# Memory and its keys turned by VectorE and carried through DRAM, and h written in block order

## The chip, the cores and the metric

The kernel runs on one core of a Trainium2 chip. Its time is that of one execution on the device, in microseconds; several executions are timed, and their median counts. One further execution is recorded by the hardware profiler, and the rows in this document come from such records.

## The reference, cut to what matters

Two layers over x (256 rows of 1024, float32), with a memory of 256 rows of 1024 that both layers attend to:

```
for i in range(2):
    x = x + 0.5 * swiglu(rmsnorm(x, ffn1_norm[i]), w_gate, w_up, w_down)   # 1024 -> 2816 -> 1024
    proj = rmsnorm(x, mix_norm[i]) @ w_in[i]           # queries, keys, values, memory queries
    mkv = rmsnorm(mem, mem_norm[i]) @ w_mem_kv[i]      # 1024 -> 2 x 256
    k_m, v_m = split(mkv)
    k_m = rmsnorm(k_m per head of 64, mem_k_norm[i])   # 4 heads
    o_m = softmax(q_m k_m' / 8) v_m
    ...                                                # 12 self heads: biased (layer 0), differential (layer 1)
    x = x + concat(o_s, o_m) @ w_out[i]
    x = x + 0.5 * swiglu(rmsnorm(x, ffn2_norm[i]), ...)
```

## The kernel before

A matrix product takes its contraction along the partitions, so everything that is multiplied has to lie with its columns on the partitions: x, memory, the gated product h, the memory keys. Every float32 operand is split into a rounded part and a rest (`hi` and `lo`), and a product is three matmuls: hi x hi, hi x lo, lo x hi (`dense`, L383, L386, L389).

**Weights.** They come in chunks of 1 MB, in one fixed order: per FFN 22 gate/up chunks and 11 down chunks; in layer 0, behind the first FFN, four chunks of the memory's key and value weights for both layers, then the mixer's. `loader` sends each chunk into one of 3 raw buffers (L270); `split_hi` (ScalarE, L302) and `split_lo` (VectorE, L314) write it into one of 4 hi/lo buffers, in quarters. A raw buffer is free when the rest is written, a hi/lo buffer when TensorE has used the chunk for the last time. In the kernel before, the memory itself is a chunk too (1 MB, ahead of the down stage's last three), not split.

**Order of the work.** All instructions of all engines are put in order when the kernel is built, by a planner (`Flow`): threads (Python generators) yield a time or a condition, and a clock with fixed costs (0.216 us a matmul, and so on) says when each goes on. The splits and the loader are idle threads, taken when no other is ready. What the planner gives is the order in each engine's queue; the chip then runs each queue as its data come. `at[0]` is the number of the chunk that TensorE works on. Small loads go through a list (`later`): the loader sends one of them behind each chunk from number 5 on, and `loaded` waits until that is done and 8 us more:

```
if i > 4 and late_done[0] < len(late_loads):
    dst, src = late_loads[late_done[0]]
    late_done[0] += 1
    nc.sync.dma_start(out=dst, in_=src)
```

**Gate/up.** For each of 11 groups of 256 columns, TensorE fills two PSUM banks (`gu`, one for each 128 rows of x). `evac` applies the SiLU on ScalarE (L491), multiplies on VectorE into `h` (L494), and turns h in 32x32 blocks on VectorE into `hb` (L502). Blocks of 32 rows are then put in their places by a write to DRAM (`hd`, L508) and a read back (`hr`, L513), and split into `ht` (L519, L521) for the down stage.

**Down.** 11 chunks accumulate in four banks (`acc`); the last three (c = 8 to 10) are taken bank by bank, so that they stay in their buffers until nearly the end, while `finish` adds each finished half to x, turns it on TensorE (`xtp`), scales and splits it (`y`, `xh`, `xl`).

**Memory.** `memory_prep` is started in the first down stage, after chunk c = 6. It turns the memory chunk by 16 TensorE transposes (`mtp`, in packs), and for each layer splits it with that layer's gain into `memh` (ScalarE, L628) and `meml` (VectorE, L633). At the start of the first mixer, `memory_kv` multiplies it with the key and value weights for both layers (`kv`), normalises the keys (`kmn`, L590), turns them by TensorE (`kmtp`) and splits them into `km`. They are first used by the memory attention, at the end of the mixer (`S<-km`).

Of the kernel before, what the change touches and what calls it, by code (L numbers as in the profile page):

```python
# [12 lines left out]
F32 = mybir.dt.float32  # L13
# [4 lines left out]
ALU = mybir.AluOpType  # L18
# [124 lines left out]
def kernel(  # L143
# [94 lines left out]


    class Chunk:  # L240
        def __init__(self, parts, mem=False):
            self.parts, self.mem = parts, mem
# [10 lines left out]
    LAT = 1.5  # L253
    at = [0]

    def add_chunk(parts, uses=8, mem=False):
        c = Chunk(parts, mem)
        c.uses = uses
        c.index = len(chunks)
        chunks.append(c)  # L260
        return c
# [25 lines left out]

    def split_hi():
        for i, c in enumerate(chunks):
            if c.mem:  # L290
                continue
            yield lambda: c.raw is not None and hl_left[0] > 0
            hl_left[0] -= 1
            yield c.early or c.arrive
            c.hi = whl.tile([P, 2048], F32R, tag="hi", name=f"hi{i}")
            c.lo = whl.tile([P, 2048], F32R, tag="lo", name=f"lo{i}")
            for q in range(4):
                if q == 2:
                    yield c.arrive
                yield lambda: flow.free["A"] <= flow.now + SLACK or i <= at[0] + AHEAD  # L300
                sl = slice(q * 512, (q + 1) * 512)
                nc.scalar.copy(out=c.hi[:, sl], in_=c.raw[:, sl])  # L302
                c.hit[q] = flow.act(512)

    def split_lo():
        for i, c in enumerate(chunks):
            if c.mem:
                continue
            for q in range(4):
                yield lambda: c.hit[q] is not None  # L310
                yield c.hit[q]
                yield lambda: flow.free["V"] <= flow.now + SLACK or i <= at[0] + AHEAD
                sl = slice(q * 512, (q + 1) * 512)
                nc.vector.tensor_sub(c.lo[:, sl], c.raw[:, sl], c.hi.bitcast(F32)[:, sl])  # L314
                c.lot[q] = flow.dve(512)
            raw_left[0] += 1
# [21 lines left out]
    def plan_ffn(l, nm, wg, wu, wd):  # L338
        gu = []
        for g in range(NG):  # L340
            ids = []
            for c in range(2):
                pieces = 2 if len(chunks) < 2 else 1
                a = cols4(wg[l], c, g * 256, 256, 0, pieces)
                b = cols4(wu[l], c, g * 256, 256, 256, pieces)
                ids.append(add_chunk([q for ab in zip(a, b) for q in ab]))
            gu.append(ids)
        plan[l, nm, "gu"] = gu
        dn = []
        for c in range(NG):  # L350
            dn.append(add_chunk(rows2(wd[l], c)))
            if (l, nm) == (0, 1) and c == NG - 4:
                plan["mem"] = add_chunk(
                    [(lambda raw: raw.rearrange("p (b d) -> p b d", b=2), mem[0].rearrange("(b p) d -> p b d", p=P))],
                    mem=True)
        plan[l, nm, "dn"] = dn

    for l in range(DEPTH):
# [119 lines left out]
    def ffn(l, nm, xt, gc_next):  # L478
# [3 lines left out]
        def evac(g, ps, end):  # L482
# [3 lines left out]
            for tb in range(2):  # L486
                yield lambda: end[tb] is not None and xt.rt[tb] is not None
                yield end[tb]
                yield g2.has(3)
                sil = g2.take([P, 256], F32, "sil")  # L490
                nc.scalar.activation(sil, ps[tb][:, 0:256], AF.Silu, scale=xt.r[tb])  # L491
                yield flow.act(256)
                h = g2.take([P, 256], F32, "h")
                nc.vector.scalar_tensor_tensor(out=h, in0=ps[tb][:, 256:512], scalar=xt.r[tb], in1=sil,  # L494
                                               op0=ALU.mult, op1=ALU.mult)
                t = flow.dve(256, 0.06)
                g2.give()
# [4 lines left out]
                nc.vector.transpose(out=hb[:, :, tb].rearrange("p b f j -> p f b j"),  # L502
                                    in_=h.rearrange("p (f i b) -> p f b i", f=2, b=4))
                t = flow.dve(256, 0.05)
                g2.give()
            yield t
# [91 lines left out]
    kvres = {}  # L598
    mrs = [const.tile([P, 1], F32, name=f"mr{tb}") for tb in range(2)]

    def memory_prep():
        c = plan["mem"]
        yield lambda: c.arrive is not None
        yield c.arrive
        yield g4.has(4 * DEPTH)
        mr = c.raw.rearrange("p (b d) -> p b d", b=2)
# [3 lines left out]
        left = [KT // 2]  # L610

        def turn_pair(i):
            yield banks.has()
            tp = bank("mtp")
            for k in range(2):
                for tb in range(2):
                    kk = 2 * i + k
                    t = turn(tp[:, 2 * k + tb, :], mr[:, tb, kk * P:(kk + 1) * P])
            yield t
            parts = []  # L620
            for l in range(DEPTH):
                mh, ml, tt = memT[l]
                for k in range(2):
                    kk = 2 * i + k
                    g = gcol[:, GC_MEM + l * KT + kk:GC_MEM + l * KT + kk + 1]
                    src = tp[:, 2 * k:2 * k + 2, :].rearrange("p a b -> p (a b)")
                    hi = mh[kk // 4][:, kk % 4, :]
                    nc.scalar.activation(hi, src, AF.Copy, scale=g)  # L628
                    t = flow.act(256)
                    parts.append((ml[kk // 4][:, kk % 4, :], src, g, hi, tt, kk))  # L630
            yield t
            for lo, src, g, hi, tt, kk in parts:
                nc.vector.scalar_tensor_tensor(out=lo, in0=src, scalar=g, in1=hi.bitcast(F32),  # L633
                                               op0=ALU.mult, op1=ALU.subtract)
                tt[kk] = flow.dve(256, 0.06)
            banks.give()
            left[0] -= 1
            if i < KT // 2 - 2:
                yield from turn_pair(i + 2)

        for i in range(2):
            flow.spawn(turn_pair(i))
        for tb in range(2):
            ss = small([P, 2], "mss")
            for hf in range(2):
                yield lambda: flow.free["A"] <= flow.now
                nc.scalar.activation(junk, mr[:, tb, hf * 512:(hf + 1) * 512], AF.Square, accum_out=ss[:, hf:hf + 1])
                t = flow.act(512)
            yield t
            nc.vector.tensor_add(ss[:, 0:1], ss[:, 0:1], ss[:, 1:2])  # L650
            yield flow.dve(1)
            yield from rsqrt(mrs[tb], ss[:, 0:1], 1, 1.0 / D)
        yield lambda: left[0] == 0
        raw_left[0] += 1

    def split_evac(dst, src, gain):

# [14 lines left out]
    def memory_kv(l):  # L672
# [7 lines left out]
        def evac(ps, tb, t):  # L680
# [5 lines left out]
            yield banks.has()  # L686
            tp = bank("kmtp")
            for pr in range(2):
                t = turn(tp[:, pr, :], nat[:, pr * P:(pr + 1) * P])
            g2.give()  # L690
            yield t
            ts_ = slice(tb * P, (tb + 1) * P)
            kvt[0][tb] = yield from split_evac((km[:, 0, :, ts_], km[:, 1, :, ts_]), tp[:, 0:2, :],
                                               gcol[:, GC_MK + l:GC_MK + l + 1])
            banks.give()
# [643 lines left out]
```

## Time and profile before

| what | value |
|---|---|
| median of 3 runs | 976.7 us (974.52 to 978.5) |
| profiled execution | 974.42 us, span 972.6 us |
| TensorE busy | 964.5 us (99%), 4576 matmuls and transposes |
| VectorE busy | 687.3 us (71%) |
| ScalarE busy | 543.0 us (56%) |
| GpSimd busy | 59.9 us (6%) |
| moved by DMA | 200.86 MB, mean 207 GB/s |

The span runs from the first instruction to the last; the execution's time has some 2 us more around it. Matmuls overlap, so that a busy TensorE is read from the distance between their starts. The granted TensorE clock was 1.00 throughout.

### The profile page before, as it was taken

The numbers are of one execution on the slowest core, as the hardware profiler recorded it, in microseconds if no ns is written. First come the engines' busy times: TensorE is split into PE (matmuls) and PEld (weight loads), VectorE is DVE, ScalarE is ACT, GpSimd is POOL, SyncE is SP. The second block draws the span as 40 slices with busy tenths as digits, with TensorE's granted clock in tenths as the row PEclk, the third lists the DMA queues.
The fourth block names the chain that finished last, engine by engine and source line by source line (L and its number), as shares of the span: only waits on it lengthen the run. The fifth ranks groups of instructions, "written<-read, shape, count | busy, mean of one in ns | idle before, by whom it ended". The sixth has DMA issues, their size and how long they took to land.

```text
span 972.6 us, 13036 instructions
## 1 busy us (share of the span) xinstructions
PE 964.5 (99%) x4576; PEld 791.3 (81%) x4576; DVE 687.3 (71%) x1397; ACT 543.0 (56%) x1159; POOL 59.9 (6%) x65
## 2 busy tenths in 40 slices
PE   9999999999999999999999999999999999999998
PEld 7888888887777888888888888888787788888886
DVE  7776775887777877765477676644989886776641
ACT  6654544766685645454445555443677764655540
POOL 0000000022210000000000000000344100000000
PEclk9999999999999999999999999999999999999999
DMA  9988766485525587777638877764641368887631
GB/s 295 313 257 249 255 221 209 159 260 173 173 88 174 161 255 237 245 237 231 209 124 264 253 236 236 255 204 141 203 145 47 128 197 256 258 258 250 231 130 44
DMA packets 162332, 200.86 MB, mean 207 GB/s; under 512 B 7321, under 2 KB 137946, under 8 KB 162266
## 3 DMA queue, kind: packets, MB, share of 16 engines
q1 hardware_dynamic: 162266, 200.03, 64.2%
q8 instruction: 36, 0.59, 0.3%
q14 instruction: 30, 0.25, 0.1%
HBM read 187.42 MB, written 12.58 MB: 206 GB/s over the span
## 4 chain that ended last, share of the span: by engine, by line
PE 94%; DVE 3%; ACT 1%; DMA 0%; issue 0%; SPq 0%; ACTq 0%
PE gu L383 16%; PE gu L389 16%; PE gu L386 16%; PE acc L386 10%; PE acc L389 10%; PE acc L383 10%; PE pj L389 3%; PE pj L383 3%; PE pj L386 3%; PE xtp L396 1%; PE AV L1062 1%; PE ptp L396 1%; PE S L981 1%; DVE lo L314 1%; PE kv L389 1%; PE kv L386 1%
## 5 line engine op out<-in xcount | busy, mean ns | idle before, releaser
L314 DVE TENSOR_TENSOR lo<-raw,hi 128x512 fp32r<-128x512 f32 x656 | 416.8, 683 | 189.2 <-ACT hi L302 189.0
L302 ACT CAST hi<-raw 128x512 fp32r<-128x512 f32 x656 | 366.5, 618 | 289.2 <-PE gu L389 165.0
L389 PE MATMUL gu<-hi,xl 128*128 128x512 f32 x704 | 274.3, 390 | 0.0
L383 PE MATMUL gu<-hi,xh 128*128 128x512 f32 x704 | 274.1, 389 | 0.0
L386 PE MATMUL gu<-lo,xh 128*128 128x512 f32 x704 | 274.0, 389 | 0.0
L389 PEld LDWEIGHTS gu<-hi,xl 128*128 128x128 f32 x704 | 132.1, 188 | 27.6
L383 PEld LDWEIGHTS gu<-hi,xh 128*128 128x128 f32 x704 | 132.1, 188 | 27.3
L386 PEld LDWEIGHTS gu<-lo,xh 128*128 128x128 f32 x704 | 132.1, 188 | 27.2
L383 PE MATMUL acc<-hi,ht 128*128 128x512 f32 x352 | 137.7, 391 | 0.0
L386 PE MATMUL acc<-lo,ht 128*128 128x512 f32 x352 | 137.4, 390 | 0.2 <-DVE lo L314 0.2
L389 PE MATMUL acc<-hi,ht 128*128 128x512 f32 x352 | 137.4, 390 | 0.0
L386 PEld LDWEIGHTS acc<-lo,ht 128*128 128x128 f32 x352 | 66.1, 188 | 14.1 <-DVE lo L314 0.7
L389 PEld LDWEIGHTS acc<-hi,ht 128*128 128x128 f32 x352 | 66.1, 188 | 13.7
L383 PEld LDWEIGHTS acc<-hi,ht 128*128 128x128 f32 x352 | 66.1, 188 | 13.5
L389 PE MATMUL pj<-hi,xl 128*128 128x512 f32 x160 | 64.7, 404 | 0.0
L386 PE MATMUL pj<-lo,xh 128*128 128x512 f32 x160 | 63.6, 398 | 0.0
L383 PE MATMUL pj<-hi,xh 128*128 128x512 f32 x160 | 63.6, 398 | 0.0
L502 DVE STREAM_TRANSPOSE hb<-h 128x256 f32<-128x256 f32 x88 | 55.5, 630 | 1.3
L491 ACT ACTIVATE sil<-gu,xr 128x256 f32<-128x256 f32 x88 | 41.5, 471 | 21.6 <-PE gu L389 21.6
L494 DVE SCALAR_TENSOR_TENSOR h<-gu,xr,sil 128x256 f32<-128x256 f32 x88 | 42.2, 479 | 2.3
L521 DVE TENSOR_TENSOR ht<-hr,ht 128x512 fp32r<-128x512 f32 x44 | 30.1, 683 | 14.3 <-ACT ht L519 14.3
L403 POOL TENSOR_TENSOR hf<-v,nhalf 128x8 f32<-128x8 f32 (+1 forms) x20 | 30.9, 1544 | 106.0 <-DVE v L401 87.6
(167 smaller groups left out, 801.4 us busy)
## 6 DMA issues: line engine op xcount, KB each, us to landing
raw<-in_ffn_w_down_dram SPq DMA_DIRECT2D x44, 1024.0 KB, 5.3
raw<-in_ffn_w_gate_dram SPq DMA_DIRECT2D x86, 512.0 KB, 4.1
raw<-in_ffn_w_up_dram SPq DMA_DIRECT2D x86, 512.0 KB, 5.3
raw<-in_w_in_dram SPq DMA_DIRECT2D x32, 512.0 KB, 4.1
hd<-hb SPq DMA_DIRECT2D x44, 256.0 KB, 2.0
hr<-hd SPq DMA_DIRECT2D x44, 256.0 KB, 5.2
raw<-in_w_out_dram SPq DMA_DIRECT2D x8, 1024.0 KB, 4.9
raw<-in_w_mem_kv_dram SPq DMA_DIRECT2D x4, 1024.0 KB, 7.5
```

The lines of the kernel that those rows point to most:

```text
L302: nc.scalar.copy(out=c.hi[:, sl], in_=c.raw[:, sl])
L314: nc.vector.tensor_sub(c.lo[:, sl], c.raw[:, sl], c.hi.bitcast(F32)[:, sl])
L383: nc.tensor.matmul(out=ps, lhsT=xh, rhs=wh, start=start, stop=False)
L386: nc.tensor.matmul(out=ps, lhsT=xh, rhs=wl, start=False, stop=False)
L389: nc.tensor.matmul(out=ps, lhsT=xl, rhs=wh, start=False, stop=stop)
L396: nc.tensor.transpose(out=dst, in_=src, identity=flip if flipped else ident)
L403: nc.gpsimd.tensor_tensor(out=dst, in0=v[:, :n], in1=nhalf[:, :n], op=ALU.pow)
L491: nc.scalar.activation(sil, ps[tb][:, 0:256], AF.Silu, scale=xt.r[tb])
L494: nc.vector.scalar_tensor_tensor(out=h, in0=ps[tb][:, 256:512], scalar=xt.r[tb], in1=sil, op0=ALU.mult, op1=ALU.mult)
L502: nc.vector.transpose(out=hb[:, :, tb].rearrange("p b f j -> p f b j"), in_=h.rearrange("p (f i b) -> p f b i", f=2, b=4))
L521: nc.vector.tensor_sub(lo, src, hi.bitcast(F32))
L981: nc.tensor.matmul(out=ss[e][:, pr, :nk], lhsT=q[rows, pr, :], rhs=k[rows, pr, :], start=i == 0, stop=i == len(passes) - 1)
```

## The change

- Memory is no longer a chunk. A thread `memory_turn`, started at the beginning, takes it in four quarters of 256 columns through the list of small loads, each after the one before: squares for the norm on ScalarE, the turn in 32x32 blocks on VectorE, a write to DRAM (`md`).
- `memory_prep` waits until all four are written, reads them back (`mr`) and splits them from SBUF; the rest is written in two halves of 128 columns for each slice.
- The normalised keys are turned in the same way (`kb`, `kd`, `kr`), both halves of the rows together.
- h is written in block order: the product's output has a stride instead of the turn's input, and column 8 i + 2 b + k goes to partition 4 i + b of slice k (before, column 128 k + 4 i + b); the down weights are loaded to match, two neighbouring rows on one partition. Memory and keys are turned in the order that h had before.

```diff
-            dn.append(add_chunk(rows2(wd[l], c)))
-            if (l, nm) == (0, 1) and c == NG - 4:
-                plan["mem"] = add_chunk(
...
+            dn.append(add_chunk(pairs2(wd[l], c)))
...
+    def pairs2(w, r):
+        return [(lambda raw: k2(raw), w[r * 256:(r + 1) * 256, :].rearrange("(p k) n -> p k n", k=2))]
...
-                h = g2.take([P, 256], F32, "h")
-                nc.vector.scalar_tensor_tensor(out=h, in0=ps[tb][:, 256:512], scalar=xt.r[tb], in1=sil,
+                h = g2.take([P, 8, 32], F32, "h")
+                nc.vector.scalar_tensor_tensor(out=h.rearrange("p q i -> p i q"),
+                                               in0=ps[tb][:, 256:512].rearrange("p (i q) -> p i q", q=8),
+                                               scalar=xt.r[tb], in1=sil.rearrange("p (i q) -> p i q", q=8),
...
-                nc.vector.transpose(out=hb[:, :, tb].rearrange("p b f j -> p f b j"),
-                                    in_=h.rearrange("p (f i b) -> p f b i", f=2, b=4))
+                nc.vector.transpose(out=hb[:, :, tb].rearrange("p b k j -> p b (k j)"),
+                                    in_=h.rearrange("p (b k) i -> p b (k i)", k=2))
...
+    def through_dram(src, tag, n):
+        d = dram.tile([4, 32, 4, P], F32, tag=tag, name=tag, bufs=n)
+        nc.sync.dma_start(out=d.rearrange("a i b x -> (a i) (b x)"), in_=src.rearrange("p b t k j -> p (b t k j)"))
+        return d
+
+    def from_dram(d, name):
+        r = g2.take([P, 4, 2, 2, 32], F32, name)
+        nc.sync.dma_start(out=r.rearrange("p a t k j -> p a (t k j)"), in_=d.rearrange("a i b x -> (i b) a x"))
+        return r
+
+    def turn_blocks(dst, src):
+        nc.vector.transpose(out=dst.rearrange("p b k j -> p k b j"),
+                            in_=src.rearrange("p (k i b) -> p k b i", k=2, b=4))
+        return flow.dve(256, 0.35)
+
+    def memory_turn():
+        yield lambda: at[0] >= 8
+        ss = const.tile([P, 2, 4], F32, name="mss")
+        for q in range(4):
+            yield g2.has(8)
+            m = g2.take([P, 2, 256], F32, "mem")
+            later(m, mem[0, :, q * 256:(q + 1) * 256].rearrange("(b p) d -> p b d", p=P))
+            yield from loaded()
+            yield g2.has(3)
+            xb = g2.take([P, 4, 2, 2, 32], F32, "mb")
+            for tb in range(2):
+                nc.scalar.activation(junk[:, 0:256], m[:, tb], AF.Square, accum_out=ss[:, tb, q:q + 1])
+                flow.act(256, 0.1)
+                yield lambda: flow.free["V"] <= flow.now
+                t = turn_blocks(xb[:, :, tb], m[:, tb])
+            yield t
+            g2.give()
+            memd.append(through_dram(xb, "md", 4))
+            yield flow.now + 3.0
+            g2.give()
...
     def memory_prep():
+        yield lambda: len(memd) == 4
         yield g4.has(4 * DEPTH)
...
+        for q in range(4):
+            yield g2.has(2)
+            r = from_dram(memd[q], "mr")
+            yield flow.now + (4.5 if q == 0 else 0.5)
             for l in range(DEPTH):
                 for k in range(2):
+                    parts.append((l, 2 * q + k, r[:, :, :, k, :].rearrange("p a t j -> p t a j"), q, l == k == 1))
+        for l, kk, src, q, last in parts:
...
+            yield lambda: flow.free["A"] <= flow.now + SLACK
+            nc.scalar.activation(hi, src, AF.Copy, scale=g)
+            yield flow.act(256)
+            yield lambda: flow.free["V"] <= flow.now + SLACK
+            for tb in range(2):
+                nc.vector.scalar_tensor_tensor(out=lo[:, tb], in0=src[:, tb], scalar=g, in1=hi.bitcast(F32)[:, tb],
                                                op0=ALU.mult, op1=ALU.subtract)
...
+    flow.spawn(memory_turn())
```

In `memory_kv`'s `evac`, the two TensorE transposes of each half and their bank give way to `turn_blocks`, one `through_dram` and one `from_dram` for both halves, and splits from SBUF, again with the rest in two halves.

More of the change, by code (lines that the diff above doesn't have):

```diff
@@ L254, with add_chunk @@
     at = [0]
-    def add_chunk(parts, uses=8, mem=False):
-        c = Chunk(parts, mem)
+    def add_chunk(parts, uses=8):
+        c = Chunk(parts)
         c.uses = uses
@@ L599 @@
     mrs = [const.tile([P, 1], F32, name=f"mr{tb}") for tb in range(2)]
+    memd = []
+    def through_dram(src, tag, n):
[30 more added lines that the diff above has]
+            g2.give()
+        s2 = small([P, 2], "mss2")
+        nc.vector.tensor_reduce(out=s2, in_=ss, axis=AX.X, op=ALU.add)
+        yield flow.dve(8)
+        for tb in range(2):
+            yield from rsqrt(mrs[tb], s2[:, tb:tb + 1], 1, 1.0 / D)
     def memory_prep():
-        c = plan["mem"]
-        yield lambda: c.arrive is not None
-        yield c.arrive
+        yield lambda: len(memd) == 4
         yield g4.has(4 * DEPTH)
-        mr = c.raw.rearrange("p (b d) -> p b d", b=2)
         for l in range(DEPTH):
@@ L609, in memory_prep @@
                        [g4.take([P, 4, SEQ], F32R, f"meml{l}{i}") for i in range(2)], [None] * KT)
[L610 to L620, printed above, removed]
+        parts = []
+        for q in range(4):
+            yield g2.has(2)
+            r = from_dram(memd[q], "mr")
+            yield flow.now + (4.5 if q == 0 else 0.5)
@@ L685, in evac @@
             banks.give()
[L686 to L689, printed above, removed]
+            if tb == 0:
+                yield g2.has()
+                kb.append(g2.take([P, 4, 2, 2, 32], F32, "kb"))
+            else:
+                yield lambda: len(kb) > 0
+            t = turn_blocks(kb[0][:, :, tb], nat)
             g2.give()
             yield t
[L692 to L695, printed above, removed]
+            done.append(tb)
+            if len(done) < 2:
+                return
+            d = through_dram(kb[0], "kd", 2)
+            yield flow.now + 4.0
+            g2.give()
+            yield g2.has()
+            r = from_dram(d, "kr")
+            yield flow.now + 5.0
+            for pr in range(2):
+                src = r[:, :, :, pr, :].rearrange("p a t j -> p t a j")
+                hi, lo = (km[:, i, pr, :].rearrange("p (t a j) -> p t a j", t=2, a=4) for i in range(2))
+                g = gcol[:, GC_MK + l:GC_MK + l + 1]
+                nc.scalar.activation(hi, src, AF.Copy, scale=g)
+                yield flow.act(256)
+                for j in range(2):
+                    nc.vector.scalar_tensor_tensor(out=lo[:, j], in0=src[:, j], scalar=g, in1=hi.bitcast(F32)[:, j],
+                                                   op0=ALU.mult, op1=ALU.subtract)
+                    t = flow.dve(128, 0.06)
+            g2.give()
+            kvt[0][0] = kvt[0][1] = t
+        kb, done = [], []
         flow.until(banks.has(2))
```

47 lines of the change are left out of this document (9 added, 38 removed).

## The prediction

> **What bounds the kernel now.** I read the page's busy line first, then the groups by line, then who waits for whom, then the queues in order of time.
>
> ```profile
> span 972.6 us, 13036 instructions
> PE 964.5 (99%) x4576; PEld 791.3 (81%) x4576; DVE 687.3 (71%) x1397; ACT 543.0 (56%) x1159; POOL 59.9 (6%) x65
> ...
> L314 DVE TENSOR_TENSOR lo<-raw,hi 128x512 fp32r<-128x512 f32 x656 | 416.8, 683 | 189.2 <-ACT hi L302 189.0
> ...
> L389 PE MATMUL gu<-hi,xl 128*128 128x512 f32 x704 | 274.3, 390 | 0.0
> ```
>
> TensorE is busy for 99% of the span, and its costliest group has 0.0 us of idle time ahead of it. So time is won in two ways only: fewer TensorE instructions, or fewer of the few stalls. VectorE (71%) has slack on average, and waits itself:
>
> ```profile
> DVE lo L314 <- ACT hi L302: 189.0, 118, 2.9
> ACT hi L302 <- PE gu L389: 165.0, 78, 2.9
> ```
>
> The weight splits wait for TensorE to free a buffer, not the other way round. A faster VectorE instruction in a gate/up stage therefore buys nothing; a later one in a stretch without that lead can stall TensorE.
>
> **What the change removes.** 24 TensorE transposes go: 16 of memory (`mtp`: packs of 8, 4 and 4) and 8 of the keys (`kmtp`: 4 packs of 2).
>
> ```profile
> 167.54 0.39 PE L386 MATMUL acc<-lo,ht 128*128 128x512 f32 x1
> 167.77 0.39 PE L389 MATMUL acc<-hi,ht 128*128 128x512 f32 x1
> 168.00 1.03 PE L396 MATMUL mtp<-ident,raw 128*128 128x128 f32 x8
> 168.79 0.48 PE L383 MATMUL acc<-hi,ht 128*128 128x512 f32 x1
> 169.10 0.39 PE L386 MATMUL acc<-lo,ht 128*128 128x512 f32 x1
> ...
> 173.01 0.60 PE L396 MATMUL mtp<-ident,raw 128*128 128x128 f32 x4
> 173.37 0.47 PE L386 MATMUL acc<-lo,ht 128*128 128x512 f32 x1
> ...
> 205.44 0.38 PE L396 MATMUL kmtp<-ident,kmn 128*128 128x128 f32 x2
> 205.58 0.47 PE L389 MATMUL kv<-hi,meml 128*128 128x512 f32 x1
> ```
>
> Starts are 0.23 apart in the dense stream (167.54, 167.77, 168.00). The pack of 8 takes 168.79 - 168.00 = 0.79, and the matmul after it 0.31 to the next start instead of 0.23: 0.87 in all. A pack of 4: 0.36 + 0.08 = 0.44. A pack of 2: 0.14 + 0.08 = 0.22. Sum 0.87 + 2 x 0.44 + 4 x 0.22 = 2.6 us, all on the path.
>
> With them goes one small stall. The memory splits sit on ScalarE and VectorE just ahead of a table load and of the weight halves for the end of the down stage:
>
> ```profile
> 175.24 1.28 ACT L574 ACT_TABLE_LOAD   x1
> ```
>
> ```profile
> 178.70 0.40 PE L383 MATMUL acc<-hi,ht 128*128 128x512 f32 x1
> 179.34 0.50 PE L386 MATMUL acc<-lo,ht 128*128 128x512 f32 x1 [0.24 <-DVE lo L314]
> 179.68 0.40 PE L389 MATMUL acc<-hi,ht 128*128 128x512 f32 x1
> ```
>
> 0.64 and 0.34 between starts instead of 0.23 each: 0.5 us. What is late next there is the table load alone, with no memory work ahead of it, so I count the 0.5 as won. Removed: 3.1 us.
>
> **What it adds, and when.** The name says "early", but the transfer list decides. The loader sends one small transfer behind each weight chunk from chunk 5 on; 20 stand on the list before memory (12 gain rows, 4 lambda, 4 rope), so `at[0] >= 8` (some 50 us) opens nothing: the first memory quarter goes behind chunk 25.
>
> ```profile
> 113.98 0.46 SPq L285 DMA_DIRECT2D gqk<-in_b_k_norm_dram  x1
> ...
> 116.97 0.38 SPq L270 DMA_DIRECT2D raw<-in_ffn_w_down_dram  x1
> ...
> 134.94 0.37 SPq L270 DMA_DIRECT2D raw<-in_ffn_w_down_dram  x1
> ...
> 149.72 11.28 SPq L270 DMA_DIRECT2D raw<-in_ffn_w_down_dram  x3
> 166.04 17.25 SPq L270 DMA_DIRECT2D raw<-in_w_mem_kv_dram  x4
> ```
>
> The last of the 20 follows chunk 24 at 113.98, so quarter 0 goes out at 117.4, behind chunk 25. Each further quarter is put on the list only when the one before is turned: 8 (the wait in the code, counted on the planner's clock, which runs about 5% fast: 0.216 a matmul against 0.227) + about 1.5 to 3.5 for two squares, two turns and VectorE's gaps + 3.0, together 13.5 to 15.5 us, and then it waits for the next chunk. Chunks go out some 5.4 us apart, so that is three chunks, sometimes four: chunk 28 (134.94), then 31 (149.72, the memory chunk no longer ahead of it) or 32 (some 155), then 34 (166.0) or 35 (some 171). Quarter 3 is turned and its write issued 10 to 11 us later: 177 or 182. Only then may `memory_prep` begin: 4.5 + 3 x 0.5, stretched as above, so that the first split comes at about 183.5 or 188. In the kernel before, VectorE's part of them began at 170.2 and was done by 177:
>
> ```profile
> L633 DVE SCALAR_TENSOR_TENSOR meml<-mtp,gcol,memh x16: 474/476/484, 170.2 to 176.4; 128x256 fp32r<-128x256 f32 x16
> ```
>
> When they are needed, and what VectorE has to do by then:
>
> ```profile
> L383 PE MATMUL kv<-hi,memh x32: 387/389/477, 193.6 to 216.0; 128*128 128x512 f32 x32
> ```
>
> ```profile
> 191.27 0.69 DVE L314 TENSOR_TENSOR lo<-raw,hi 128x512 fp32r<-128x512 f32 x1 [0.96 <-ACT hi L302]
> ```
>
> ```profile
> 180.00:205.00 25.00, 25.00 (x120) 20.64 (x119) 21.03 (x47) 16.20 (x36) 3.89 (x5) 1.00 0.80 261
> 205.00:225.00 20.00, 20.00 (x93) 16.38 (x92) 15.40 (x41) 11.56 (x24) 4.60 (x6) 1.00 0.81 272
> ```
>
> ```profile
> L432 DVE TENSOR_TENSOR xl<-y,xh 128x512 fp32r<-128x512 f32 x24 | 16.5, 687 | 4.8 <-ACT xh L430 4.5
> ...
> L1108 DVE SCALAR_TENSOR_TENSOR pe<-pe,cf 128x128 f32<-128x128 f32 x6 | 2.3, 420 | 0.1
> ...
> L789 DVE SCALAR_TENSOR_TENSOR ropeC<-gqk,ropew 128x32 f32<-128x32 f32 x8 | 1.4, 174 | 0.0
> ```
>
> The memory projection `kv` starts at 193.6 and, 2.3 us of the removed work lying ahead of it (0.87 + 2 x 0.44 + 0.5), would start at 191.3. It asks for k-slice 7 after 7 x 0.68 = 4.8 us and one pack of transposes (0.4): 196.5. Behind 188 VectorE has by then to do: 14 of the 16 memory splits (layer 1's last two come after), each now in two 128-wide halves. A half of that shape is nowhere in the trace: the same operation takes 174 ns at 32 and 476 at 256, so 303 on the line between, which I take; the one 128-wide row says 420, and half of 476 is 238. 28 x 0.303 = 8.5 us (6.7 and 11.8 by the ends). Chunk 34's halves, which wait for a buffer that the down stage frees late (191.27 before, so about 189): 4 x 0.683 = 2.7. And x, y and xl of the last halves of x, up to five of 0.687 = 3.4. Sum 11.2 to 14.6, so done at 199.2 to 202.6 against 196.5; VectorE was busy 21.03 of 25 us in this stretch already, so nothing absorbs it. The stall is 2.7 to 6.1 if all lies ahead of the matmul, less where the x work or a split falls behind or starts on data landed early: ScalarE and VectorE run ahead of the plan when they can, by a microsecond or two. I take 3.5, and keep 0 and 9 (420 ns halves) as ends. That price returns what was removed.
>
> **The rest, costed at nothing, and its cover.** The turning itself (8 x 0.63, squares beside it), 4 writes, 4 read-backs:
>
> ```profile
> L502 DVE STREAM_TRANSPOSE hb<-h 128x256 f32<-128x256 f32 x88 | 55.5, 630 | 1.3
> ```
>
> ```profile
> hd<-hb SPq DMA_DIRECT2D x44, 256.0 KB, 2.0
> hr<-hd SPq DMA_DIRECT2D x44, 256.0 KB, 5.2
> ```
>
> ```profile
> 129.00:189.00 60.00, 59.76 (x275) 49.21 (x274) 40.58 (x104) 33.54 (x71) 1.10 (x2) 1.00 0.59 196
> ```
>
> 5.0 us more on VectorE where it is busy 40.58 of 60, DMA at 0.59: hidden. On SyncE's queue the writes wait for the turn, and the next weight load behind them for as long; weights lead by three raw buffers there, so nothing. The four reads go ahead of the first bias load, for which TensorE waits nowhere; the two powers for memory's norm move behind the last turn on a POOL that is busy 1.1 of 60 us. The memory chunk leaves a raw buffer free: weights come earlier, which is not what they wait for. Keys: 4 turns (2.5) and 8 halves for 4 whole ones (0.5 more), VectorE 15.4 + 3.0 of 20 in 205 to 225; write, read and splits end near 232, and the first score on `km` was at 289.1:
>
> ```profile
> L981 PE MATMUL S<-km,qmT x48: 274/278/383, 289.1 to 764.2; 64*128 64x256 f32 x48
> ```
>
> 57 us of cover; if it were gone, about 10 us a layer. h in block order: 88 turns now read and write runs instead of every fourth element, 88 products write with a stride. Between -0.2 and +0.2 us each way, -18 to +18 us of VectorE in four gate/up stages of about 120 us, where it waits for ScalarE: nothing. w_down's rows in pairs make longer runs in loads that wait for buffers: nothing.
>
> Sum against the profiled execution's 974.4 us (span 972.6 and 1.8 around it): -3.1 + 3.5 = +0.4, 974.8. The median of the runs, 976.7, lies 2.3 above that execution, so 977.1 on its scale.
>
> The page "VectorE: DVE Perf Modes" of the Trainium skill, under "Rules for kernel authors", would keep a 128x128 transpose on TensorE where PSUM will do as its place, which speaks against this change. By that rule the 3.1 us are no gain worth having; here the row of TensorE at 99% speaks for the change and the window of VectorE at 21.03 of 25 for the rule.
>
> **Rivals.** *Hidden after all*: the quarters ride on chunks 28, 31, 34, splits start at 183.5 and end by 196.5. For it: the third step misses chunk 31 by a few tenths at most. Against it: VectorE's load between 183 and 196. -3.1 to -1.5: 973.6 to 975.2. *Quarter 3 on chunk 36* (about 176.5): splits begin at 193 to 194, 8.5 + 2 us of them after 193: a stall of 7 to 8, +4.3, 981. *Missing chunk 36*: chunk 37's buffer is freed only by chunk 34's halves, near 192. Then the write is at 202, the splits begin at 208.5, and TensorE stands from 191.3 on: 17 + 2 - 3 = +16, 993. The point from which this decides is quarter 3 being listed after 176. Against it: it takes two or three slips of a chunk. *Faster elsewhere*: with 8 fewer packs and freer PSUM banks the first mixer is ordered anew and loses some of its own stalls, -5: 971.7; but those stalls come to little, TensorE being at 10.0 of 10 in nearly all windows.
>
> **How the numbers follow.** Forecast (splits from 188, a stall of 2 to 5) 0.42; hidden 0.30; chunk 36 0.13; miss 0.07; faster elsewhere 0.08. Half a per cent (4.9 us) is about what a measurement here tells from no change. Forecast and hidden lie within it, and half of the chunk-36 case and part of each tail: 0.72. Slower 0.19, faster 0.09. The likeliest case alone (a stall of 2 to 5, and a microsecond of spread between runs) holds 974.5 to 980; with hidden and chunk 36 and the spread of runs it is 972.5 to 982.
>
> **What would show it.** TensorE counts 24 fewer; `raw<-mem` is gone and `mem` goes out in quarters near 117, 135, 150 to 155, 166 to 172. `meml` starts at 183 to 189 rather than 170.2, and a wait of `kv` for `meml` or `lo` of some 3 us stands near 193 to 200: that is the step most in doubt. If the splits end before 191, or the first quarter goes out near 50, the stall is gone and so is my sum. A wait over 10 us there is the miss. The turn of `hb` away from 630 ns with no change in the gate/up stages bears out their cover; a wait of TensorE for `km` would refute mine for the keys.

## The result, and the profile after

| | median | range |
|---|---|---|
| before | 976.39 us (4 runs) | 974.52 to 978.5 |
| changed kernel | 980.98 us (4 runs) | 980.3 to 981.9 |

The ratio on record is 1.0059 (95% interval 1.0044 to 1.0074): the changed kernel is slower. By the two medians it is 4.6 us (1.0047). The four runs of the kernel before lie 4 us apart, though; against its later groups of runs (medians of 974.7 to 975.1) the loss is about 6 us (1.0060 to 1.0064). The profiled execution of the changed kernel took 981.15 us, of which 978.5 are span, 5.9 more than the profiled execution before. First the page of the changed kernel (busy times, then two of the groups):

```profile
span 978.5 us, 13054 instructions
PE 965.3 (99%) x4552; PEld 789.3 (81%) x4552; DVE 696.5 (71%) x1428; ACT 545.0 (56%) x1167; POOL 59.5 (6%) x65
...
L489 DVE SCALAR_TENSOR_TENSOR h<-gu,xr,sil 128x256 f32<-128x256 f32 x88 | 60.9, 692 | 2.3
...
L499 DVE STREAM_TRANSPOSE hb<-h 128x256 f32<-128x256 f32 x88 | 38.5, 438 | 1.2
```

The 24 transposes are gone (4576 to 4552), and yet the span is longer. TensorE still reads as 99% busy, so the loss can't be seen in this line. It shows when the first matmul of each stage is looked up. The rows of the memory projection `kv` and of the mixer's projection `pj` that follows it, in the changed kernel (duration min/median/max, then first and last start):

```profile
L378 PE MATMUL kv<-hi,memh x32: 389/389/796, 191.5 to 222.9; 128*128 128x512 f32 x32
```

```profile
L378 PE MATMUL pj<-hi,xh x160: 387/389/504, 223.6 to 759.5; 128*128 128x512 f32 x160
```

and `pj` in the kernel before (its `kv` began at 193.6):

```profile
L383 PE MATMUL pj<-hi,xh x160: 387/389/504, 216.7 to 753.0; 128*128 128x512 f32 x160
```

`kv` begins 2.1 us earlier than before (191.5 against 193.6), and `pj` begins 6.9 later (223.6 against 216.7). The stretch of `kv` has grown from 23.0 to 32.1 us; from `pj` to the end the changed kernel wins back 1.0 (6.9 to 5.9). All of the loss lies in these 32 us. What TensorE waited for, by the chain of waits (in all, times, longest):

```profile
PE kv L378 <- ACT memh L661: 2.4, 2, 1.6
PE kv L384 <- DVE meml L665: 2.3, 4, 1.0
```

That is 4.7 us of idle time. From start to start, the six gaps in which these waits lie are together 7.0 us longer than the 0.23 each of the dense stream. Some 3 us more lie between them, most of it where TensorE ran at half its clock (0.43 from start to start). Windows of 2 us in that stretch (us, then busy time of TensorE, weight loads, VectorE, ScalarE and GpSimd, the granted clock, DMA share and GB/s):

```profile
194.00:196.00 2.00, 0.73 (x2) 0.30 (x2) 2.00 (x6) 2.00 (x6) 0.00 (x0) 1.00 0.04 8
196.00:198.00 2.00, 1.42 (x3) 0.63 (x3) 2.00 (x7) 2.00 (x7) 0.00 (x0) 0.66 0.33 62
198.00:200.00 2.00, 0.80 (x1) 0.29 (x1) 1.97 (x8) 2.00 (x6) 0.55 (x1) 0.50 1.04 299
...
204.00:206.00 2.00, 1.62 (x4) 0.80 (x4) 2.00 (x7) 0.00 (x0) 0.00 (x0) 0.50 1.07 377
```

VectorE is busy 1.97 to 2.00 of 2.00 throughout. Now SyncE's queue, to see why the memory was late (start, length, issue):

```profile
117.67 0.43 SPq L285 DMA_DIRECT2D mem<-in_mem_dram  x1
...
135.53 0.43 SPq L285 DMA_DIRECT2D mem<-in_mem_dram  x1
...
155.88 0.43 SPq L285 DMA_DIRECT2D mem<-in_mem_dram  x1
...
172.11 0.50 SPq L285 DMA_DIRECT2D mem<-in_mem_dram  x1
...
179.81 0.34 SPq L602 DMA_DIRECT2D md<-mb  x1
180.20 3.60 SPq L607 DMA_DIRECT2D mr<-md  x4
```

The four quarters are 16 to 20 us apart, the last is written at 179.8, and the read-backs go out right behind it. What VectorE made of them: first all the rests of memory, then its groups in the window from 189 to 207, then the end of that window in order of time.

```profile
L665 DVE SCALAR_TENSOR_TENSOR meml<-mr,gcol,memh x32: 332/341/348, 189.6 to 207.6; 128x128 fp32r<-128x128 f32 x32
```

```profile
L665 DVE SCALAR_TENSOR_TENSOR meml<-mr,gcol,memh 128x128 fp32r<-128x128 f32 x29 | 8.5, 341 | 0.0
L310 DVE TENSOR_TENSOR lo<-raw,hi 128x512 fp32r<-128x512 f32 x12 | 8.1, 678 | 0.0
L422 DVE TENSOR_TENSOR y<-xtp,gcol 128x512 f32<-128x512 f32 x2 | 1.4, 682 | 0.3 <-PE xtp L391 0.3
L427 DVE TENSOR_TENSOR xl<-y,xh 128x512 fp32r<-128x512 f32 x2 | 1.4, 678 | 0.0
```

```profile
198.19 0.67 DVE L310 TENSOR_TENSOR lo<-raw,hi 128x512 fp32r<-128x512 f32 x1
...
199.04 0.60 DVE L665 SCALAR_TENSOR_TENSOR meml<-mr,gcol,memh 128x128 fp32r<-128x128 f32 x2
199.56 1.28 DVE L310 TENSOR_TENSOR lo<-raw,hi 128x512 fp32r<-128x512 f32 x2
200.77 0.61 DVE L665 SCALAR_TENSOR_TENSOR meml<-mr,gcol,memh 128x128 fp32r<-128x128 f32 x2
201.30 0.68 DVE L310 TENSOR_TENSOR lo<-raw,hi 128x512 fp32r<-128x512 f32 x1
201.90 0.60 DVE L665 SCALAR_TENSOR_TENSOR meml<-mr,gcol,memh 128x128 fp32r<-128x128 f32 x2
202.42 0.68 DVE L310 TENSOR_TENSOR lo<-raw,hi 128x512 fp32r<-128x512 f32 x1
203.03 1.13 DVE L665 SCALAR_TENSOR_TENSOR meml<-mr,gcol,memh 128x128 fp32r<-128x128 f32 x4
204.07 0.68 DVE L310 TENSOR_TENSOR lo<-raw,hi 128x512 fp32r<-128x512 f32 x1
204.68 1.13 DVE L665 SCALAR_TENSOR_TENSOR meml<-mr,gcol,memh 128x128 fp32r<-128x128 f32 x4
205.73 0.68 DVE L310 TENSOR_TENSOR lo<-raw,hi 128x512 fp32r<-128x512 f32 x1
206.33 1.65 DVE L665 SCALAR_TENSOR_TENSOR meml<-mr,gcol,memh 128x128 fp32r<-128x128 f32 x6
```

VectorE takes one split of memory (two halves), then one weight half, and so on. Twelve weight halves stand in this window. Four belong to chunk 34, which the running `kv` bank needs at once. The other eight, counted from the end, belong to chunks 35 and 36, which are needed only by layer 1's banks, the third and fourth of `kv` (from 212.7 on).

The two halves of a split hold memory's rows 0 to 127 and 128 to 255, and the first bank takes rows 0 to 127 alone. So of the pair at 201.90 it waits for the first half (ready at 202.24) and not for the second (202.50): the product starts at 202.29. Its last product needs k-slice 7 of layer 0, the 14th split, and so the 27th half. This is the first of the six that start at 206.33, ready at 206.67. TensorE, whose products just before it ran below full clock, starts the product that needs it at 206.97:

```profile
202.29 0.79 PE L384 MATMUL kv<-hi,meml 128*128 128x512 f32 x1 [0.59 <-DVE meml L665]
...
206.62 0.51 PE L381 MATMUL kv<-lo,memh 128*128 128x512 f32 x1
206.97 0.40 PE L384 MATMUL kv<-hi,meml 128*128 128x512 f32 x1
```

ScalarE's copies (`memh`) are interleaved in the same way, and TensorE waits for two of them; but the first eight are issued by 198.48, and the other eight follow from 199.92 in a row, some 0.4 apart, so the fourteenth is done near 202.4, 4.3 us before VectorE's half. VectorE's queue ends last.

So the first theory: memory comes too late to VectorE's queue, and there it is interleaved one for one with weight halves that nobody needs yet. The rivals: the new keys or h cost the time; the clock that was halved costs it; lateness alone costs all of it, whatever the order.

### The profile page after: what moved, and what is told of

Read it like the earlier page. It is cut to its first block, busy times and chain, and to the rows that moved or that the text cites. A ratio compares the mean times of both kernels' runs of the same rounds, so it can differ in the third digit from the quotient of the medians.

```text
span 978.5 us, 13054 instructions
## 1 busy us (share of the span) xinstructions
PE 965.3 (99%) x4552; PEld 789.3 (81%) x4552; DVE 696.5 (71%) x1428; ACT 545.0 (56%) x1167; POOL 59.5 (6%) x65
## 4 chain that ended last, share of the span: by engine, by line
PE 92%; DVE 6%; ACT 1%; DMA 0%; issue 0%; SPq 0%; ACTq 0%
PE gu L384 16%; PE gu L378 16%; PE gu L381 16%; PE acc L378 10%; PE acc L384 10%; PE acc L381 10%; PE pj L384 3%; PE pj L381 3%; PE pj L378 2%; DVE lo L310 2%; PE xtp L391 1%; PE S L1016 1%; PE AV L1097 1%; PE ptp L391 1%; DVE meml L665 1%; PE kv L384 1%
## 5 line engine op out<-in xcount | busy, mean ns | idle before, releaser
L384 PEld LDWEIGHTS gu<-hi,xl 128*128 128x128 f32 x704 | 132.1, 188 | 27.5
L381 PEld LDWEIGHTS gu<-lo,xh 128*128 128x128 f32 x704 | 132.1, 188 | 27.4
L489 DVE SCALAR_TENSOR_TENSOR h<-gu,xr,sil 128x256 f32<-128x256 f32 x88 | 60.9, 692 | 2.3
L499 DVE STREAM_TRANSPOSE hb<-h 128x256 f32<-128x256 f32 x88 | 38.5, 438 | 1.2
```

What stands on the lines that cost most here:

```text
L381: nc.tensor.matmul(out=ps, lhsT=xh, rhs=wl, start=False, stop=False)
L384: nc.tensor.matmul(out=ps, lhsT=xl, rhs=wh, start=False, stop=stop)
L489: nc.vector.scalar_tensor_tensor(out=h.rearrange("p q i -> p i q"), in0=ps[tb][:, 256:512].rearrange("p (i q) -> p i q", q=8), scalar=xt.r ...
L499: nc.vector.transpose(out=hb[:, :, tb].rearrange("p b k j -> p b (k j)"), in_=h.rearrange("p (b k) i -> p b (k i)", k=2))
```

## The experiments

The table puts the runs side by side. "kv" is the time from the first `kv` matmul to the first `pj` matmul in the profiled execution, "4th write" the issue of the last `md` write, "splits" the first and last start of `meml`. Before: 23.0 us. The kernel before had medians of 974.74, 975.14 and 975.05 us in the three groups of runs.

| run | median us | ratio [95%] | kv us | 4th write | splits |
|---|---|---|---|---|---|
| changed kernel | 980.98 | 1.0059 [1.0044, 1.0074] | 32.1 | 179.8 | 189.6 to 207.6 |
| early | 971.24 | 0.9963 [0.9949, 0.9977] | 22.2 | 121.7 | 179.4 to 201.7 |
| hold weights | 977.61 | 1.0033 [1.0021, 1.0046] | 27.5 | 181.0 | 190.7 to 204.2 |
| layer 0 first | 974.20 | 0.9998 [0.9988, 1.0007] | 25.2 | 180.7 | 190.4 to 211.1 |
| keys and h alone | 974.03 | 0.9995 [0.9986, 1.0004] | 22.2 | - | - |
| h alone | 974.96 | 0.9994 [0.9986, 1.0003] | 23.0 | - | - |
| before, late | 978.56 | 1.0035 [1.0024, 1.0047] | 27.4 | - | 188.9 to 196.8 |
| fill | 980.82 | 1.0058 [1.0042, 1.0073] | 32.4 | 180.0 | 189.8 to 208.3 |
| from chunk 21 | 981.13 | 1.0055 [1.0040, 1.0070] | 31.9 | 180.1 | 189.8 to 207.9 |
| from chunk 20 | 976.91 | 1.0017 [1.0003, 1.0030] | 27.2 | 174.2 | 183.4 to 203.1 |
| from chunk 19 | 972.17 | 0.9965 [0.9954, 0.9977] | 22.2 | 170.8 | 179.0 to 200.3 |

### Memory really early

The quarters are loaded directly, from chunk 8 on, and not through the list.

```diff
-            later(m, mem[0, :, q * 256:(q + 1) * 256].rearrange("(b p) d -> p b d", p=P))
-            yield from loaded()
+            nc.sync.dma_start(out=m, in_=mem[0, :, q * 256:(q + 1) * 256].rearrange("(b p) d -> p b d", p=P))
+            yield flow.now + 8.0
```

> The changed kernel with memory's four loads issued at once when their thread asks for them (from chunk 8 on, some 50 us), not through the list of small loads; all else as changed. Theory L (late): the cost is that the memory splits come late and queue on VectorE while kv waits. Then kv waits for memory less than 0.5 us in all (changed kernel: 9.9 us between 191.5 and 207), and the 2.6 us of transposes and 0.5 us of stall are won: 973.3 us against 976.4 before, ratio 0.996 to 0.998. Rival W (work): 32 half splits and the turns are simply more VectorE work, wherever they lie: the stall moves to the end of the down stage and the time stays over 977. Rival E (elsewhere): the stride in h or the keys' way through DRAM costs it: 980 or more, with kv free of waits.

Measured: 971.24 us, 0.9963, 3.5 us faster than before. No wait of `kv` is left. Its writes and its rests:

```profile
L602 SPq DMA_DIRECT2D md<-mb x4: 354/378/825, 68.2 to 121.7; - x4
```

```profile
L665 DVE SCALAR_TENSOR_TENSOR meml<-mr,gcol,memh x32: 341/345/347, 179.4 to 201.7; 128x128 fp32r<-128x128 f32 x32
```

The fourth write stands at 121.7 in place of 179.8. (This profiled execution ran 4.2 us behind from its first stage on, as the last section tells, so its `kv` begins at 195.7.) Between the first `acc` matmul and `kv` lie 61.3 us, against 63.7 before: 2.4 won, 1.8 of memory's transposes and the rest the small stall. `kv` took 22.2 in place of 23.0: 0.8, the keys' transposes. With nothing late, the change gives 3.2 us in the trace. So the idea of the change works; its place in time is what fails.

### Weights held back

Chunks 35 and 36 are split only after the last split of memory, the rounded parts on ScalarE and the rests on VectorE alike.

```diff
+            if i in (NG * 3 + 2, NG * 3 + 3):
+                yield lambda: memory_split[0]
```

> The changed kernel with the splits of the last two memory weight chunks (35 and 36) held back until all memory splits are issued. Theory L with the order as its size: 8 weight halves of 0.6 us that nobody needs yet stand between the memory splits on VectorE; without them the last split that the first kv bank needs ends 4.8 us earlier (206.9 to about 202), kv waits about 5 us instead of 9.9, and the time is 976 us, ratio 0.999 to 1.001. If the end is set by the reads from DRAM or by ScalarE instead, it stays at 981.

Measured: 977.61 us, 1.0033; `kv` fell from 32.1 to 27.5, 4.6 less. The 4.8 expected of it came, but the whole kernel gained less than that. The waits say why:

```profile
PE kv L388 <- DVE meml L669: 3.6, 4, 2.0
PE qktp L395 <- DVE qkn L591: 1.6, 1, 1.6
```

The second line is new: with the weights of the later chunks late, VectorE's work for the mixer comes late as well, and the mixer (from `pj` to the next `acc`) took 72.9 us against 71.1. So 1.8 us are given back, and the 976 us that I had expected did not come. The eight halves explain about half of the stall (4.6 of 9.8); holding back the other work is not the way to have it. The run relieves ScalarE's queue as well and does not tell the two engines apart. That VectorE's is the one that ends last is read from the traces: here TensorE waits for `meml` alone.

### Layer 0 first

The same splits, with the eight of layer 0 ahead of those of layer 1.

```diff
-        for l, kk, src, q, last in parts:
+        for l, kk, src, q, last in sorted(parts, key=lambda v: v[0]):
```

> The changed kernel with layer 0's eight memory splits ahead of layer 1's, the same instructions in another order. Theory L: the last split that the first kv bank needs is the 8th and not the 14th, about 5.6 us earlier (201.3, where the 8th ended): kv waits about 4.3 us, 975.5 us, ratio 0.998 to 1.000. Rival W: the same work, the same time, 981; or layer 1's projection then waits for what layer 0's no longer waits for.

Measured: 974.20 us, 0.9998: the whole loss of the changed kernel is gone, although the fourth write is as late as in the changed kernel (180.7). `kv` took 25.2 us, and this is left of the waits:

```profile
PE kv L384 <- DVE meml L665: 1.3, 3, 0.8
```

The first bank needs eight splits. In the order by quarters fourteen have to be done, because six of layer 1 stand between. My prediction had the fourteen as a count and did not see that six of them were not needed, nor the second halves of the other eight. This run, too, changes the order on both engines. The stall of some 3 us (25.2 less 22.2) eats what the transposes give.

### Keys and h alone, and h alone

In the first, memory is the old chunk, turned by TensorE; in the second, the kernel before has only the new h and the down weights in pairs.

```diff
+            if (l, nm) == (0, 1) and c == NG - 4:
+                plan["mem"] = add_chunk(
...
-    flow.spawn(memory_turn())
```

> The changed kernel with memory as it was before (a chunk of its own, 16 TensorE transposes, 16 whole splits); the keys still go through DRAM and h is still in block order. Theory L: all of the loss is memory's, so this is the kernel before less 8 transposes of the keys (0.9 us): 975.5 us, ratio 0.998 to 1.000, kv without waits. Rival E: the loss stays, 979 or more.

> The kernel before with h in block order and the down weights in pairs, nothing else. In the changed kernel the product h took 692 ns for 479 and its turn 438 for 630, so VectorE's work is the same within 2 us over the span. Theory L: no change, ratio 0.9985 to 1.0015. Rival E: the stride costs something, 1.002 or more.

Measured: 974.03 us (0.9995) and 974.96 us (0.9994). Both intervals hold 1. With the keys `kv` took 22.2 us and with h alone 23.0: the keys give their 0.8 us, and h gives and costs nothing. Neither is the cause; the loss is memory's alone.

### The kernel before, made late

Memory turned by TensorE as before, but started 17 us later on the planner's clock, so that its rests begin when those of the changed kernel do.

```diff
+        yield flow.now + LATE    # LATE = 17.0
```

> The kernel before, with its memory transposes and splits held back by 17 us on the planner's clock (some 18 us of time: first split near 188 as in the changed kernel, not 170); memory is still turned by TensorE and split whole. Theory L: lateness alone does it, without DRAM, VectorE turns or halves: kv waits for memory by 5 to 10 us, 980 to 985 us, ratio 1.005 to 1.010. If it needs the halves and the way through DRAM, the time stays within 2 us of before.

Measured: 978.56 us, 1.0035: slower, as expected, but by 3.4 us and not by 5 to 10. Its rests, and its waits:

```profile
L635 DVE SCALAR_TENSOR_TENSOR meml<-mtp,gcol,memh x16: 472/474/479, 188.9 to 196.8; 128x256 fp32r<-128x256 f32 x16
```

```profile
PE kmtp L397 <- DVE kmn L591: 2.1, 2, 1.4
PE kv L387 <- DVE lo L315: 1.6, 1, 1.6
```

Sixteen whole rests are done 8 us after the first has begun, since a pack brings four or eight in a row and no weight half comes between. TensorE waits for a weight half and for the keys' product that were pushed back, not for memory.

But the edit does more than make the splits late. In this kernel memory stands in one of the three raw buffers and keeps it while it is held back (its last square ends at 203.2). So the last chunk of `kv`'s weights is asked for at 200.53, and not by 183 as in the kernel before, and ScalarE waits for it:

```profile
200.53 0.37 SPq L271 DMA_DIRECT2D raw<-in_w_mem_kv_dram  x1
```

```profile
205.84 2.18 ACT L303 CAST hi<-raw 128x512 fp32r<-128x512 f32 x4 [2.63 <-DMA raw<-in_w_mem_kv_dram]
```

The first wait for the keys' product (1.4) stands behind the rests of this chunk. So the 3.4 us are lateness and a held buffer together, and what lateness alone costs is not shown. Even both together fall short of the changed kernel's loss (1.0035 against 1.0059), and the run with layer 0 first is as late and loses nothing: lateness alone does not explain all of it.

### The clock

In the changed kernel, 21 idle matmuls (42 instructions in the trace) fill the gaps between the products of the first `kv` bank. They write to the second bank, which is started afresh afterwards.

```diff
+                    if l == tb == 0:
+                        for _ in range((0, 5, 3, 8, 2, 3, 0, 0)[kk]):
+                            nc.tensor.matmul(out=ps[1][:, 0:P], lhsT=ident, rhs=ident, start=True, stop=True)
```

> The changed kernel with 21 idle matmuls of 128 columns (about 0.2 us each, into a bank that is overwritten later) put between kv's first products, where TensorE waits, to keep it busy. In the changed kernel the granted clock was 0.5 in 198 to 206 us, and 17 matmuls there took 0.43 us instead of 0.23. If that halving adds to the stall, 2 to 3 us come back: 978. If VectorE's queue sets the end, as the last split at 206.9 beside TensorE's 206.97 says, the clock stays at 1.0 and the time at 981, ratio 1.004 to 1.007.

Measured: 980.82 us, 1.0058, as slow as the changed kernel. The same windows in this run:

```profile
198.00:200.00 2.00, 1.91 (x14) 1.43 (x13) 1.97 (x8) 2.00 (x6) 0.08 (x1) 1.00 0.92 271
204.00:206.00 2.00, 1.71 (x11) 1.17 (x9) 2.00 (x8) 0.00 (x0) 0.17 (x1) 1.00 1.05 363
```

The clock stays at 1.00 and nothing is won. The slow matmuls (14 that start below full clock in the changed kernel, not the 17 of the expectation) stood in time that VectorE set anyway. There, the first bank's last product started at 206.97; its half was ready at 206.67, and the products that waited for a half of memory started 0.05 to 0.06 behind it. So at most some 0.3 us are the clock's. The fillers have a price of their own: they put off a turn of x, for which VectorE waited 0.34 us, and a gain smaller than that would not show. Without the windows of VectorE (1.97 to 2.00 of 2.00 here in both kernels) one could have put 5 us, all that is not in the waits, down to the clock.

### How early is early enough

The direct load again, but from chunk 21, 20 or 19 in place of 8. From chunk 21 on it was meant to bring the write to 176.

```diff
-        yield lambda: at[0] >= 8
+        yield lambda: at[0] >= 21    # and 20, 19
```

> The changed kernel with memory's loads issued at once as in e1_early, but asked for from chunk 21 on and not from chunk 8: the fourth write near 176 (179.8 in the changed kernel, near 105 in e1_early), first split near 183. Theory L as a dose: kv waits some 4 to 5 us, half of the changed kernel's 9.9: 976 us, ratio 1.000 to 1.003. If the list of small loads itself or the loads' place among the weight chunks is what costs, it is as fast as e1_early, 0.997.

> As e8_middle, but asked for from chunk 20 on. The four steps took 14 us each there and the fourth write came at 180.1, no earlier than in the changed kernel, so that run moved nothing. One chunk (5.5 us) earlier: fourth write near 174.5, first split near 182 to 184, before the last two halves of x. Theory L: 6 to 8 of the 32 halves fit into VectorE's free time ahead of 189, kv waits 4 to 6 us, 976 us, ratio 1.000 to 1.003. If the place of the memory loads in the queue is what costs, it is as slow as e8_middle.

> As e9_from20, one chunk earlier again: fourth write near 169, first split near 176 to 178. Theory L: VectorE has some 5 us free in 178 to 189, so 16 to 20 halves are done by 189, kv waits 0 to 2 us, 972 us, ratio 0.996 to 0.999.

Measured: 981.13 (1.0055), 976.91 (1.0017) and 972.17 us (0.9965). The first did not do what it was meant to: its quarters went out 12 to 16 us apart (126.7, 139.9, 156.2, 168.5), and the last write stands at 180.1, where the changed kernel has it. So it moved nothing, and its expectation missed (which also puts the fourth write of the early kernel near 105; it stands at 121.7). It does show that a direct load that ends as late as the list does is as slow, so that the list harms only by the lateness. The other two carry the curve. Their writes and rests, from chunk 20 and from chunk 19:

```profile
L602 SPq DMA_DIRECT2D md<-mb x4: 326/326/338, 129.9 to 174.2; - x4
```

```profile
L602 SPq DMA_DIRECT2D md<-mb x4: 326/333/425, 125.7 to 170.8; - x4
```

```profile
L665 DVE SCALAR_TENSOR_TENSOR meml<-mr,gcol,memh 128x128 fp32r<-128x128 f32 x10 | 3.0, 345 | 0.0
```

```profile
L665 DVE SCALAR_TENSOR_TENSOR meml<-mr,gcol,memh 128x128 fp32r<-128x128 f32 x19 | 5.5, 345 | 0.0
```

The last two lines are the groups from 179 to 189: with the write at 174.2, ten halves have begun by 189, and 5.0 us of stall remain (27.2 less the 22.2 that `kv` takes without one); with 170.8, nineteen have begun and there is no stall. In the changed kernel none had begun by 189, and the stall was 9.8. In the run from chunk 20 the clock fell too, for 3.4 us, but it adds little: the first bank's last product started at 201.62, right behind its half of memory (ready at 201.56), and only the three starts behind it were slow, 0.6 us in all. And VectorE is as full as ever where nothing is lost. The window from 189 to 199 of the kernel from chunk 19:

```profile
189.00:199.00 10.00, 10.00 (x50) 8.31 (x49) 9.98 (x26) 9.88 (x23) 0.90 (x2) 1.00 0.21 62
```

VectorE 9.98 of 10, TensorE 10.00 of 10. A full VectorE does no harm as long as what TensorE needs next is done in time. The kernels early and from chunk 19 are both faster than the kernel before and the changed one; from 171 to 174 the gain turns to a loss.

## Why the prediction went wrong

I forecast 977.1 us, a rise of 0.4, with a range of 972.5 to 982; it became 980.98, a rise of 4.6. The time lies in the range, and it meets the case of the quarter on chunk 36 by its size (981), but that is chance: that case's mechanism was not the one that came, since quarter 3 went out at 172.1, on chunk 35, as forecast.

- **What is removed: right.** 3.1 us by the rows of before, 3.2 in the trace of the early kernel (2.4 ahead of `kv`, 0.8 in it), 2.9 and 3.5 by the medians of the two kernels without a stall.
- **The transfer list: right.** First quarter at 117.67 (117.4 forecast), then 135.53, 155.88 and 172.11, the slower of the two chains I gave; the fourth write at 179.8, between 177 and 182. `kv` began at 191.5 (191.3 forecast). The first `memh` began at 187.2 and the first `meml` at 189.6, against 188.
- **The price of the stall: wrong.** This is the step that failed. I took 3.5 us, from a list that gave 2.7 to 6.1, with ends at 0 and 9; it was 9.8 (32.1 less 22.2), beyond the upper end. Two things in that term were wrong. *The list was short.* It held chunk 34's four halves and not the eight of chunks 35 and 36, which the planner puts in between one for one. In the trace, two neighbouring weight halves start 0.60 apart, so the eight are 4.8 us; holding them back took 4.6 off. *The discount had no row behind it.* I went below the middle of the list (4.4) for work that would run ahead or fall behind. Nothing ran ahead: from 190 on VectorE was busy 1.97 to 2.00 of every 2.00 us, and ScalarE 2.00 until 202.
- **The list redone with measured spacing.** Instructions start closer than their durations: halves of memory 0.26 apart, weight halves and the x work 0.60. 28 x 0.26 + 4 x 0.60 + 5 x 0.60 = 12.7, from 189.6: 202.3. With the eight extra, 4.8, it is 207.1; the trace has 206.9 for the 28th half (of the five steps of x, four stood there). The bank waits for the 27th, 0.3 earlier. The half split that no row showed was 341 ns and not 303, but in the queue it took 0.26, so that my figure was too high and not too low. So the list as I had it gives a stall of 202.3 - 196.5 = 5.8, near its own upper end, and with it 976.7 - 3.1 + 5.8 = 979.4. The eight halves add 4.8: 10.6 for the 9.8 measured. On that scale the sum -3.1 + 9.8 gives a rise of 6.7 where the two medians show 4.6. The profiled executions lie 5.9 apart, and the changed kernel wins 1.0 back after `pj`; the 976.7 from which I started lies 1.6 to 2.0 above the later medians of the same kernel.
- **The rival "hidden after all"** would not have been hidden by its own numbers: it had splits from 183.5 on, and with splits from 183.4 the kernel from chunk 20 still stalled for 5.0. It takes 179.
- **Keys: right.** No wait for `km`. The splits end at 241.3, 9 us later than the 232 I gave, and the first score on `km` starts at 296.1, so that 55 us of cover were left. **h: right.** The product went from 479 to 692 ns and the turn from 630 to 438, +18.7 and -16.9 us of VectorE, about the 18 that I had given as the bound of each, and the run with h alone shows no effect.
- **The rule cited against the change** (the Trainium skill, page "VectorE: DVE Perf Modes", "Rules for kernel authors") is not borne out by the runs in which memory is early: there the move away from TensorE gave about 3 us. In the changed kernel the time comes out on the rule's side (1.0059), since the work came back as a wait.

## What to carry to other kernels

When a step is moved to an engine's queue close to its deadline, sum up everything that the scheduler will put in that queue ahead of the last needed instruction, work for later stages too, and take no discount that no row shows. If the sum misses the deadline, first change the order (what the next consumer needs goes first: here one sort took the ratio from 1.0059 to 0.9998), then the start. An early condition in the code is not an early transfer: find the queue that it stands in, and count its places.

## What the hardware showed that I had not expected

- The granted clock fell to 0.50 without TensorE ever standing still for long: it was busy 0.73 of 2.00 us from 194 to 196, with single waits of 0.81 and 0.97, and 0.50 then held for 10.24 us, in both runs with this stall. The Trainium skill, page "TensorE: Matmul & The Clock Gate", section "What's actually happening", knows two states, half and full, and ties the half one to an idle window of about 3.4 us; the value 0.50 agrees, but no idle window of that length is in the trace. In the run with the weights held back the clock stayed at 1.00 over a stretch no busier than that:

```profile
196.00:198.00 2.00, 0.52 (x2) 0.48 (x3) 2.00 (x7) 1.93 (x5) 0.00 (x0) 1.00 0.00 0
```

  What separates the two is open. The stretches at 0.50 in these traces, the end of the span left out, last 3.41, 3.41, 6.83, 10.24 and 10.24 us: one, one, two, three and three times 3.41. By the run with the idle matmuls and the start of the bank's last product, the halved clock cost the changed kernel no more than some 0.3 us.
- A VectorE product that writes with a stride takes 692 ns in place of 479 at 128x256, and a turn that reads neighbours in place of every fourth element 438 in place of 630. The two nearly cancel.
- The profiled execution of the early kernel stands 4.2 us behind that of the changed kernel when the down stage begins (134.4 against 130.2): x landed late, TensorE waited 3.2 us for it (1.5 in the changed kernel), and the clock was at 0.5 for 6.8 us, until 15.9. Its 974.54 us stand beside a median of 971.24. One profiled execution can be off by as much as the effect looked for here, so stages were compared from mark to mark and not from the start.

Not tried: rests of memory split whole (256 wide) from SBUF, and the early load together with layer 0 first. The two would tell whether anything is left in VectorE's queue once nothing waits for it. Nor was lateness tried without the held raw buffer, an order that puts the eight first halves of layer 0 ahead of all else, or either engine's queue apart from the other's.
